# A two-layer streaming step: priority of PSUM copies for the steps between dependent products of indexer and attention

## The chip, the cores and the metric

The kernel runs on one core of a Trainium2 chip. The engines are PE (TensorE, matrix products; PEld is its weight load), DVE (VectorE), ACT (ScalarE), POOL (GpSimd) and SP (SyncE, which issues loads). The metric is the device time of one execution in microseconds.

## The reference

The program computes one inference step of a hybrid encoder with 2 layers of width 1024, for 512 prompt positions and 32 positions of a running stream with 1024 cached ones, in float32. A layer is:

```python
h = rms_norm(x, g_mix)
z = h @ w_in
...
q = rope(rms_norm(q.reshape(B, T, N_HEADS, HEAD_DIM), q_gain), pos)
...
qi = rope(qi.reshape(B, T, N_IDX, IDX_DIM), pos)
ki = rope(ki[:, :, None, :], pos)[:, :, 0, :]
wi = wi * IDX_W_SCALE
...
x = x + jnp.concatenate([y_a, y_b, y_c], axis=-1) @ w_out
hf = rms_norm(x, g_ffn)
x = x + jnp.square(jax.nn.relu(hf @ w_up)) @ w_down
```

`y_a` is a spatial gate and `y_b` a short convolution; `y_c` is attention over the positions that an indexer picks:

```python
logits = jax.nn.relu(jnp.einsum('bqnd,bsd->bqns', qi, ki_all).astype(jnp.float32))
iscore = jnp.einsum('bqn,bqns->bqs', wi.astype(jnp.float32), logits)
...
_, sel = lax.top_k(iscore, k_top)
...
p = jax.nn.softmax(s, axis=-1)
o = jnp.einsum('bqhgk,bqkhd->bqhgd', p.astype(v_sel.dtype), v_sel)
```

There are 8 indexer heads of 32, 8 attention heads of 64 that share 4 key heads, and `k_top` is 128 for the prompt and 256 of 1056 for the running stream.

## The kernel before, in words

Positions are cut into blocks b = 0 to 3 of 128 prompt positions and b = 4, the 32 of the running stream (called the sample). A float32 product is made of three products of split operands, hi*hi, lo*hi and hi*lo (lines 258 to 260), so each weight tile is loaded by SP (`raw`), cast on ACT into `hi` (L226) and subtracted into `lo` on DVE or POOL (L227). Inputs and weights of a layer come in this order: the indexer's columns of `w_in`, then q (two halves, split on POOL), k, v (split on POOL), the mixers' columns, `w_out`, and the feed-forward part.

The indexer loops over the five blocks. `tok_gemm` gives a block's 296 columns in PSUM; DVE rotates them (L574) and adds the halves (L577); ACT and DVE split keys (`ks`, L584 and L586) and queries (`qs`, L598 and L600); PE transposes them and ACT copies them out (L590, L592, L608). For blocks 1 to 3 there follow eight products, one a head (L612), each with a Relu on ACT into a buffer of the group "tt", of which there are four (L614), and an accumulation with the head's weight on DVE (L616 for the first head, L618 for the others). For block 4 the sum over heads is a second product on PE: its weights `wsel` are transposed and copied by DVE in four pieces (L638), then three column ranges each take two products (L644), a Relu (L646) and two products with `wsel` (L647), and a copy (L648).

After that come the products for q, k and v, with rope (L456, L458), sums of squares (L661, L662), adds (L687, L706) and transposes whose copies are at L693 and L720. The masks of blocks 1 to 3 are made on DVE by 16 rounds of MAX8 and MATCH_REPLACE (L465, L466), that of the sample by a search digit by digit. `attend(b)` then makes, for two heads at a time, two score products (L754) into the two PSUM tiles of the group "l"; DVE adds the mask and takes the row maximum in one instruction (L761), which frees the tile; ACT takes the exponential; PE transposes the probabilities, ACT copies them (L780), and PE multiplies by the values (L784). The mixers' products (L428, L683 and others) are ready at the same time and lie between these.

What sets the order is the scheduler of the tile framework. Each instruction has a priority, its place in the program, and of the instructions whose inputs it takes as ready each engine gets the one with the lowest number. Two blocks of code shift that number for what is issued in them. Each engine's instructions stand in the order that results.

```python
PREP = -1000000
EVAC = -2000000
...
prep = Shift(tc, PREP)
evac = Shift(tc, EVAC)
```

`prep` is round loads, casts and splits of weights (L226, L227), so they go ahead of all plain work; `evac` is round copies out of PSUM behind the large products (L571, L660, L683, L703, L728 and others), and goes ahead of both. Steps named above that have neither keep the priority of their place: L577, the splits of `ks` and `qs`, the Relus, the whole branch of block 4, the row maximum and the copies of transposes.

Of the kernel before, what the change touches and what calls it, by code (L numbers as in the profile page):

```python
# [16 lines left out]
NT = 512  # L17
NS = 32
PAST = 1024
# [36 lines left out]
def kernel(  # L56
# [20 lines left out]
    def nm(s):  # L77
        cnt[0] += 1
        return f"{s}_{cnt[0]}"
# [16 lines left out]
    def psum(tag):  # L96
        return pp.tile([128, 512], F32, tag=tag, name=nm("ps" + tag), bufs=PBUFS[tag])
# [293 lines left out]
    for l in range(depth):  # L391
# [162 lines left out]
        for b in range(5):  # L554
# [22 lines left out]
            nc.vector.tensor_tensor(t1[r], t1[r], t2[r], op=ALU.add)  # L577
# [4 lines left out]
            ks = sp.tile([128, 4, 32], F32R, tag="ks", name=nm("ks"), bufs=1)  # L582
            for a in range(2):
                nc.scalar.copy(ks[r, a, :], t1[r, 256:288])  # L584
            for a in range(2):
                nc.vector.tensor_tensor(ks[r, 2 + a, :], t1[r, 256:288], ks[r, 0, :].bitcast(F32), op=ALU.subtract)  # L586
            pt = psum("l")
            tr(pt[:, :nr], ks[r].rearrange("p a e -> p (a e)"), idr[r, r])
            if b < 4:
                nc.scalar.copy(kiTp[:, b * 128:b * 128 + 128], pt[:, :128])  # L590
            else:
                nc.scalar.copy(kiTs[:, PAST:SK], pt[:, :32])  # L592
# [4 lines left out]
            for a in range(2):  # L597
                nc.scalar.copy(qs[r, :, 2 * a, :], qv)  # L598
            for a in range(2):
                nc.vector.tensor_tensor(qs[r, :, 2 * a + 1, :], qv, qs[r, :, 0, :].bitcast(F32), op=ALU.subtract)  # L600
            if b < 4:
                n = 128 * (b + 1)
                qiT = Q([128, 8, 128], F32R)
                for g in range(2):
                    pt = psum("l")
                    for k in range(4):
                        tr(pt[:, k * 128:k * 128 + 128], qs[:, 4 * g + k].rearrange("p a e -> p (a e)"), idr)
                    nc.scalar.copy(qiT[:, 4 * g:4 * g + 4, :].rearrange("p h t -> p (h t)"), pt)  # L608
                work = keep([128, n], f"work{b}") if b < 3 else work3
                for hd in range(8):  # L610
                    pl = psum("lld"[hd % 3])
                    nc.tensor.matmul(pl[:, :n], lhsT=qiT[:, hd, :], rhs=kiTp[:, :n], start=True, stop=True)  # L612
                    rl = T(n, "tt")
                    nc.scalar.activation(rl, pl[:, :n], AF.Relu)  # L614
                    if hd == 0:
                        nc.vector.tensor_scalar(work, rl, wi[:, 0:1], None, op0=ALU.mult)  # L616
                    else:
                        nc.vector.scalar_tensor_tensor(work, rl, wi[:, hd:hd + 1], work, op0=ALU.mult, op1=ALU.add)  # L618
                nc.vector.memset(work[0:64, n - 64:n], INADM)
                masks[b] = work  # L620
            else:
                pt = psum("l")
                for k in range(8):
                    tr(pt[:, k * 32:k * 32 + 32], qs[r, k].rearrange("p a e -> p (a e)"), idr[r, r])
                qiTs = kiTq[:, NT:]
                nc.scalar.copy(qiTs, pt[:, :256])

                dg = Q([128, 256])
                nc.vector.tensor_tensor(
                    dg[r].rearrange("p (h t) -> p h t", h=8),  # L630
                    wi[r].rearrange("p (h o) -> p h o", o=1).to_broadcast([32, 8, 32]),
                    idn[r, r].rearrange("p (o t) -> p o t", o=1).to_broadcast([32, 8, 32]), op=ALU.mult)
                wsel = keep([128, 2, 4, 32], "wsel")
                pt = psum("l")
                for g in range(2):
                    tr(pt[:, g * 32:g * 32 + 32], dg[r, g * 128:g * 128 + 128], idn[r, r])
                for a in range(4):
                    nc.vector.tensor_copy(wsel[:, :, a, :], pt[:, :64].rearrange("p (g t) -> p g t", g=2))  # L638
                work = works
                for c0, cn in ((0, 512), (512, 512), (1024, 32)):  # L640
                    pi = psum("l")
                    for g in range(2):
                        pl = psum("l")
                        nc.tensor.matmul(pl[:, :cn], lhsT=qiTs[:, g * 128:g * 128 + 128], rhs=kiTs[:, c0:c0 + cn], start=True, stop=True)  # L644
                        rl = T(cn, "tt")
                        nc.scalar.activation(rl, pl[:, :cn], AF.Relu)  # L646
                        nc.tensor.matmul(pi[:, :cn], lhsT=wsel[:, g].rearrange("p a t -> p (a t)"), rhs=rl, start=(g == 0), stop=(g == 1))  # L647
                    nc.scalar.copy(work[:, c0:c0 + cn], pi[:, :cn])  # L648
# [23 lines left out]
        for u in range(2):  # L672
            pieces = w_tok(C_Q + 256 * u, 256, ((0, 4), (4, 8)), nc.gpsimd)
            for b in range(5):
# [13 lines left out]
                if b < 4:  # L688
                    def turn_q(b=b, u=u, dst=dst):
# [3 lines left out]
                        nc.scalar.copy(qT[b][:, u].rearrange("p h t -> p (h t)"), pt[:, :256])  # L693
# [3 lines left out]
        for b in range(5):  # L697
# [16 lines left out]
            if b < 4:  # L714
                nc.gpsimd.dma_start(nk_p[l, 0, b * 128:b * 128 + 128].rearrange("t h e -> t (h e)"), kf)
                def turn_k(b=b, kf=kf):
# [3 lines left out]
                    nc.scalar.copy(kTp[:, :, b * 128:b * 128 + 128], pt[:, :256].rearrange("p (u t) -> p u t", u=2))  # L720
# [23 lines left out]
        def attend(b):  # L744
# [4 lines left out]
            def scores(u, hh):  # L749
# [7 lines left out]
                for j in range(2):  # L757
# [3 lines left out]
                    nc.vector.tensor_tensor_reduce(out=t, in0=p[j][:, :n], in1=masks[b], op0=ALU.add, op1=ALU.max, scale=1.0, scalar=-3e38, accum_out=mx[:, o])  # L761
# [10 lines left out]
            def values(u, hh, probs, po):  # L772
                for k0 in range(0, b + 1, 2):
# [6 lines left out]
                    nc.scalar.copy(t[:, :kn * 256], pt[:, :kn * 256])  # L780
# [428 lines left out]
```

## Time and profile before

| What | Value |
|---|---|
| Median of 3 runs | 1354.03 us (1351.96 to 1359.14) |
| Profiled execution | 1352.13 us |
| Its span, first to last instruction | 1350.1 us |
| Mean granted clock of PE | 0.980 of full speed |
| PE busy | 1303.9 us, 97% of the span |
| DVE busy | 1064.3 us, 79% |
| ACT busy | 748.4 us, 55% |
| POOL busy | 106.0 us, 8% |
| Share of PE in the chain that ended last | 82% |

Layer 0 runs from the start to some 675 us, layer 1 from there to the end; indexer and attention are at about 30 to 170 and 685 to 830 us. A busy PE is not PE at its peak: a product counts as busy for longer where the granted clock is lower. So the busy share is read together with the granted clock, and stage by stage. Times in the rows below are microseconds from the start of the span.

### The profile page before, as it was taken

How to read it: one execution, taken by the hardware profiler on the slowest of the kernel's cores; microseconds unless marked ns; L12 is line 12 of the kernel's file. 1: busy time of each engine (PE TensorE's matmuls, PEld its weight loads, DVE VectorE, ACT ScalarE, POOL GpSimd, SP SyncE). 2: the span in 40 equal slices, each digit the busy share in tenths (PEclk: the TensorE clock that was granted, in tenths of full speed). 3: DMA queues.
4: the chain of work that ended last, by engine and by line, in shares of the span. 5: the costliest groups of instructions: out<-in, count | busy, mean ns of one | idle time of the engine just before them, and what ended most of it. 6: DMA issues, size and time to landing. Idle time of an engine off the chain costs nothing.

```text
span 1350.1 us, 25832 instructions
## 1 busy us (share of the span) xinstructions
PE 1303.9 (97%) x10056; PEld 1212.9 (90%) x10056; DVE 1064.3 (79%) x2585; ACT 748.4 (55%) x1494; POOL 106.0 (8%) x109
## 2 busy tenths in 40 slices
PE   7888999999999999999997989999999999999998
PEld 6767886899999999999985878778999999999997
DVE  6989988657985967958989989865778679588695
ACT  5746797445634536445654469853555364463452
POOL 5213300001000000000022120000100000000000
PEclk7999899999999999999988989999999999999999
DMA  7124322223233243242221232202232323323322
GB/s 208 34 67 94 78 66 63 64 83 86 79 104 101 65 124 94 63 125 69 83 60 33 71 104 65 79 24 87 79 95 78 110 79 94 110 78 97 93 84 77
DMA packets 150801, 113.00 MB, mean 84 GB/s; under 512 B 7028, under 2 KB 147848, under 8 KB 150680
## 3 DMA queue, kind: packets, MB, share of 16 engines
q1 hardware_dynamic: 148040, 106.35, 26.4%
q0 software_dynamic: 2640, 5.01, 2.0%
q8 instruction: 79, 1.29, 0.4%
q14 instruction: 42, 0.34, 0.1%
HBM read 106.67 MB, written 4.67 MB: 82 GB/s over the span
## 4 chain that ended last, share of the span: by engine, by line
PE 82%; DVE 9%; issue 5%; DMA 2%; ACT 1%; POOL 0%; POOLq 0%; SPq 0%; DVEq 0%; ACTq 0%
PE psm L258 16%; PE psm L259 16%; PE psm L260 16%; PE psl L1076 13%; PE psd L1076 6%; PE pso L1076 3%; PE psl L754 3%; PE psx L106 2%; PE pso L784 2%; PE psd L106 1%; DMA ahi<-in_x_prompt_dram 1%; DVE lo L227 1%; PE psl L837 1%; DVE work L618 1%; DVE m L465 1%
## 5 line engine op out<-in xcount | busy, mean ns | idle before, releaser
L226 ACT CAST hi<-raw 128x1024 fp32r<-128x1024 f32 (+1 forms) x124 | 126.4, 1022 | 131.2 <-PE psm L259 75.6
L259 PE MATMUL psm<-h1lo,hi 128*128 128x288 f32 x640 | 190.2, 297 | 0.0
L258 PE MATMUL psm<-h1hi,hi 128*128 128x288 f32 x640 | 190.0, 297 | 0.1
L260 PE MATMUL psm<-h1hi,lo 128*128 128x288 f32 x640 | 189.5, 296 | 0.0
L227 DVE TENSOR_TENSOR lo<-raw,hi 128x1024 fp32r<-128x1024 f32 (+1 forms) x99 | 119.3, 1207 | 83.2 <-ACT hi L226 83.0
L258 PE MATMUL psm<-h0hi,hi 128*128 128x256 f32 x640 | 182.0, 284 | 0.0
L260 PE MATMUL psm<-h0hi,lo 128*128 128x256 f32 x640 | 181.4, 283 | 0.4 <-POOL lo L227 0.4
L259 PE MATMUL psm<-h0lo,hi 128*128 128x256 f32 x640 | 180.6, 282 | 0.0
L1076 PE MATMUL psl<-e,hi 128*128 128x272 f32 x768 | 151.5, 289 | 0.8 <-DVE x L1069 0.5
L1076 PEld LDWEIGHTS psl<-e,hi 128*128 128x128 f32 x768 | 121.5, 188 | 3.1 <-DVE x L1069 1.1
L260 PEld LDWEIGHTS psm<-h0hi,lo 128*128 128x128 f32 x640 | 120.6, 188 | 1.8 <-issue 0.9
L258 PEld LDWEIGHTS psm<-h1hi,hi 128*128 128x128 f32 x640 | 120.4, 188 | 1.4 <-issue 1.0
L259 PEld LDWEIGHTS psm<-h1lo,hi 128*128 128x128 f32 x640 | 120.3, 188 | 1.2 <-issue 1.0
L258 PEld LDWEIGHTS psm<-h0hi,hi 128*128 128x128 f32 x640 | 120.6, 189 | 0.8 <-issue 0.7
L259 PEld LDWEIGHTS psm<-h0lo,hi 128*128 128x128 f32 x640 | 120.6, 188 | 0.7 <-issue 0.7
L260 PEld LDWEIGHTS psm<-h1hi,lo 128*128 128x128 f32 x640 | 120.4, 188 | 0.6 <-issue 0.5
L243 ACT CAST hi<-t 128x512 fp32r<-128x512 f32 x128 | 78.4, 619 | 70.2 <-PE psl L1076 27.2
L227 POOL TENSOR_TENSOR lo<-raw,hi 128x1024 fp32r<-128x1024 f32 (+1 forms) x25 | 58.9, 2361 | 728.2 <-ACT hi L226 712.0
L1076 PE MATMUL psl<-e,lo 128*128 128x272 f32 x384 | 110.9, 289 | 0.0
L243 ACT CAST hi<-raw 128x512 fp32r<-128x512 f32 x96 | 59.6, 621 | 78.6 <-PE psl L1076 47.5
L244 DVE TENSOR_TENSOR lo<-t,hi 128x512 fp32r<-128x512 f32 x128 | 87.1, 687 | 8.5 <-ACT hi L243 5.0
L1048 ACT ACTIVATE t<-t 128x544 f32<-128x544 f32 x64 | 42.2, 659 | 70.0 <-DVE t L1047 70.0
(351 smaller groups left out, 3722.2 us busy)
## 6 DMA issues: line engine op xcount, KB each, us to landing
raw<-in_w_up_dram SPq DMA_DIRECT2D x64, 512.0 KB, 4.1
raw<-in_w_down_dram SPq DMA_DIRECT2D x64, 512.0 KB, 3.6
raw<-in_w_in_dram SPq DMA_DIRECT2D x36, 512.0 KB, 3.7
raw<-in_w_out_dram SPq DMA_DIRECT2D x8, 512.0 KB, 3.5
raw<-in_w_out_dram SPq DMA_DIRECT2D x32, 128.0 KB, 3.0
raw<-in_w_in_dram SPq DMA_DIRECT2D x8, 296.0 KB, 6.6
q<-in_cache_k_dram SPq DMA_DIRECT2D x4, 512.0 KB, 3.8
h1lo<-in_cache_v_dram SPq DMA_DIRECT2D x2, 1024.0 KB, 6.0
```

The costliest lines, as they stand in the source:

```text
L106: nc.tensor.transpose(out, in_, ident)
L226: nc.scalar.copy(hi, raw)
L227: (eng or nc.vector).tensor_tensor(lo, raw, hi.bitcast(F32), op=ALU.subtract)
L243: nc.scalar.copy(hi, src)
L244: nc.vector.tensor_tensor(lo, src, hi.bitcast(F32), op=ALU.subtract)
L258: nc.tensor.matmul(out, lhsT=st[0], rhs=mv[0], start=first, stop=False)
L259: nc.tensor.matmul(out, lhsT=st[0], rhs=mv[1], start=False, stop=False)
L260: nc.tensor.matmul(out, lhsT=st[1], rhs=mv[0], start=False, stop=last)
L754: nc.tensor.matmul(p[j][:, :n], lhsT=qT[b][e, u, hh, :], rhs=kTp[e, u, :n], start=True, stop=True)
L784: nc.tensor.matmul(po[64 * j:64 * j + 64, hh * 128:hh * 128 + 128], lhsT=Vp[:, k0 + k, (2 * u + j) * 64:(2 * u + j + 1) * 64], rhs=t[:, (2 ...
L1048: nc.scalar.activation(hidden[f], hidden[f], AF.Square)
L1076: nc.tensor.matmul(p[:, :EVEN], lhsT=st[a], rhs=mv[b], start=first and (k, a, b) == (0, 0, 0), stop=(k, a) == (3, 1), skip_group_check=True)
```

## The change

Steps of the indexer and the attention are put into `with evac:`. These are the add of the rope halves, both splits and their transposes and copies, the Relus of blocks 1 to 3, everything of block 4's branch, the copies of turned q and k, the row maximum of `attend`, and the copy of the transposed probabilities. The accumulations of L616 and L618, the sums of squares, the adds of q and k, the top-k and its masks keep the priority of their place, and so do `attend_sample`, the mixers and the feed-forward part. What is computed does not change. Line numbers behind the first edit shift: L577 becomes L578, L614 L619, L618 L623, L638 L644, L647 L653, L662 L668, L687 L693, L706 L713, L761 L770.

```diff
@@ -574,30 +574,33 @@
-            nc.vector.tensor_tensor(t1[r], t1[r], t2[r], op=ALU.add)
+            with evac:
+                nc.vector.tensor_tensor(t1[r], t1[r], t2[r], op=ALU.add)
...
-            ks = sp.tile([128, 4, 32], F32R, tag="ks", name=nm("ks"), bufs=1)
-            for a in range(2):
-                nc.scalar.copy(ks[r, a, :], t1[r, 256:288])
+            with evac:
+                ks = sp.tile([128, 4, 32], F32R, tag="ks", name=nm("ks"), bufs=1)
+                for a in range(2):
+                    nc.scalar.copy(ks[r, a, :], t1[r, 256:288])
...
+                if b < 4:
+                    nc.scalar.copy(kiTp[:, b * 128:b * 128 + 128], pt[:, :128])
+                else:
+                    nc.scalar.copy(kiTs[:, PAST:SK], pt[:, :32])
...
-            for a in range(2):
-                nc.scalar.copy(qs[r, :, 2 * a, :], qv)
-            for a in range(2):
-                nc.vector.tensor_tensor(qs[r, :, 2 * a + 1, :], qv, qs[r, :, 0, :].bitcast(F32), op=ALU.subtract)
+            with evac:
+                for a in range(2):
+                    nc.scalar.copy(qs[r, :, 2 * a, :], qv)
+                for a in range(2):
+                    nc.vector.tensor_tensor(qs[r, :, 2 * a + 1, :], qv, qs[r, :, 0, :].bitcast(F32), op=ALU.subtract)
@@ -605,13 +608,15 @@
-                    nc.scalar.copy(qiT[:, 4 * g:4 * g + 4, :].rearrange("p h t -> p (h t)"), pt)
+                    with evac:
+                        nc.scalar.copy(qiT[:, 4 * g:4 * g + 4, :].rearrange("p h t -> p (h t)"), pt)
...
-                    nc.scalar.activation(rl, pl[:, :n], AF.Relu)
+                    with evac:
+                        nc.scalar.activation(rl, pl[:, :n], AF.Relu)
@@ -619,33 +624,34 @@
             else:
-                pt = psum("l")
...
+                with evac:
+                    pt = psum("l")
...
+                    for a in range(4):
+                        nc.vector.tensor_copy(wsel[:, :, a, :], pt[:, :64].rearrange("p (g t) -> p g t", g=2))
...
+                            nc.scalar.activation(rl, pl[:, :cn], AF.Relu)
+                            nc.tensor.matmul(pi[:, :cn], lhsT=wsel[:, g].rearrange("p a t -> p (a t)"), rhs=rl, start=(g == 0), stop=(g == 1))
+                        nc.scalar.copy(work[:, c0:c0 + cn], pi[:, :cn])
@@ -690,7 +696,8 @@
-                        nc.scalar.copy(qT[b][:, u].rearrange("p h t -> p (h t)"), pt[:, :256])
+                        with evac:
+                            nc.scalar.copy(qT[b][:, u].rearrange("p h t -> p (h t)"), pt[:, :256])
@@ -717,7 +724,8 @@
-                    nc.scalar.copy(kTp[:, :, b * 128:b * 128 + 128], pt[:, :256].rearrange("p (u t) -> p u t", u=2))
+                    with evac:
+                        nc.scalar.copy(kTp[:, :, b * 128:b * 128 + 128], pt[:, :256].rearrange("p (u t) -> p u t", u=2))
@@ -758,7 +766,8 @@
-                    nc.vector.tensor_tensor_reduce(out=t, in0=p[j][:, :n], in1=masks[b], op0=ALU.add, op1=ALU.max, scale=1.0, scalar=-3e38, accum_out=mx[:, o])
+                    with evac:
+                        nc.vector.tensor_tensor_reduce(out=t, in0=p[j][:, :n], in1=masks[b], op0=ALU.add, op1=ALU.max, scale=1.0, scalar=-3e38, accum_out=mx[:, o])
@@ -777,7 +786,8 @@
-                    nc.scalar.copy(t[:, :kn * 256], pt[:, :kn * 256])
+                    with evac:
+                        nc.scalar.copy(t[:, :kn * 256], pt[:, :kn * 256])
```

The order of DVE in layer 0 round the copies of `wsel` (`raw` and `lo` are a weight tile, `e_44` block 3's accumulator and the sample's rotated q, `t_9..` and `psm` the rope of q), before:

```order
L618 SCALAR_TENSOR_TENSOR e_44_269<-t_695,wi_134_635,e_44_269 128x512
L638 COPY wsel_768<-psl_769 128x2x32
L618 SCALAR_TENSOR_TENSOR e_44_269<-t_700,wi_134_635,e_44_269 128x512
L456 TENSOR_TENSOR e_44_269<-psm_988,tab_59_365 32x2x2x64
L227 TENSOR_TENSOR lo<-raw_1185,hi 128x1024
L618 SCALAR_TENSOR_TENSOR e_44_269<-t_705,wi_134_635,e_44_269 128x512
L638 COPY wsel_768<-psl_769 128x2x32
L619 MEMSET e_44_269 64x64
L638 COPY wsel_768<-psl_769 128x2x32 x2
```

and with the change:

```order
L456 TENSOR_TENSOR t_979<-psm_950,tab_59_365 128x2x2x64
L458 TENSOR_TENSOR t_980<-psm_950,tab_60_368 128x2x2x32 x2
L456 TENSOR_TENSOR e_44_269<-psm_988,tab_59_365 32x2x2x64
L644 COPY wsel_768<-psl_769 128x2x32 x4
L458 TENSOR_TENSOR t_995<-psm_988,tab_60_368 32x2x2x32 x2
L623 SCALAR_TENSOR_TENSOR e_44_269<-t_690,wi_134_635,e_44_269 128x512
L227 TENSOR_TENSOR lo<-raw_1185,hi 128x1024
L623 SCALAR_TENSOR_TENSOR e_44_269<-t_695,wi_134_635,e_44_269 128x512
```

The four copies now stand together, ahead of the split and of the four last accumulations of block 3, which all stood ahead of the last copies before (the first of them just above the rows shown); adds and rope steps of q stand ahead of them.

The order of ACT in layer 1 round the first Relus of block 2 (the CAST of `raw` is a weight cast, of `psl` the copy of a transposed query), before:

```order
L226 CAST hi<-raw_8741 128x1024
L608 CAST q_8469<-psl_8470 128x512
L608 CAST q_8469<-psl_8476 128x512
L226 CAST hi<-raw_8745 128x1024
L226 CAST hi<-raw_8919 128x1024
L431 COPY t_8758<-psm_8749 128x256
L614 ACTIVATE t_8485<-psl_8483 128x384
L614 ACTIVATE t_8490<-psl_8488 128x384
L614 ACTIVATE t_8495<-psd_8493 128x384
L614 ACTIVATE t_8500<-psl_8498 128x384
```

and with the change:

```order
L619 ACTIVATE t_8400<-psl_8398 128x256
L612 CAST q_8469<-psl_8476 128x512
L619 ACTIVATE t_8485<-psl_8483 128x384
L601 CAST q_8566<-t_8549 128x8x32 x2
L619 ACTIVATE t_8490<-psl_8488 128x384
L619 ACTIVATE t_8495<-psd_8493 128x384
L226 CAST hi<-raw_8741 128x1024
L619 ACTIVATE t_8500<-psl_8498 128x384
L226 CAST hi<-raw_8745 128x1024
L431 COPY t_8758<-psm_8749 128x256
L226 CAST hi<-raw_8919 128x1024
L619 ACTIVATE t_8505<-psl_8503 128x384
```

The Relus, and splits of the next block, moved ahead of the weight casts.

The order of DVE in layer 0 at the row maxima of the first pair of score products (each is an ISA row and a read of its accumulator), before:

```order
L761 ISA t_1813,sa_1811<-psl_1806,mask_346 128x128
L761 ISA sa_1811 128x1
L227 TENSOR_TENSOR lo<-raw_2515,hi 128x1024
L458 TENSOR_TENSOR t_1380<-psm_1350,tab_63_378 128x4x32 x2
L662 TENSOR_REDUCE ss_185_814<-t_1334 128x4
L706 TENSOR_TENSOR t_1379<-t_1379,t_1380 128x256
L709 TENSOR_SCALAR sr_1339<-ss_185_814 128x12
L499 TENSOR_SCALAR ti_1597<-ti_1588 128x1
L501 TENSOR_TENSOR ti_1599<-ti_1588,bst 128x1
L762 SCALAR_TENSOR_TENSOR sa_1812<-sa_1811,rq_188_817 128x1
L662 TENSOR_REDUCE ss_186_815<-t_1384 128x4
L159 SCALAR_TENSOR_TENSOR sr_1343<-sr_1339,sr_1341 128x12
L761 ISA t_1819,sa_1811<-psl_1807,mask_346 128x128
```

and with the change:

```order
L770 ISA t_1813,sa_1811<-psl_1806,mask_346 128x128
L770 ISA sa_1811 128x1
L770 ISA t_1819,sa_1811<-psl_1807,mask_346 128x128
L770 ISA sa_1811 128x1
L227 TENSOR_TENSOR lo<-raw_2515,hi 128x1024
```

The second row maximum stood behind a weight split and nine smaller steps, and now follows the first.

## Rows read from the trace of the kernel before

**Rows 1.** Windows: busy us and instructions of PE, PEld, DVE, ACT, POOL; PEclk; DMA share, GB/s.

```profile
100.00:150.00 50.00, 45.00 (x339) 39.38 (x337) 46.85 (x166) 32.21 (x58) 18.98 (x25) 0.90 0.45 101
...
250.00:300.00 50.00, 49.71 (x419) 44.99 (x418) 27.61 (x71) 22.33 (x43) 0.00 (x0) 1.00 0.31 88
...
750.00:800.00 50.00, 44.31 (x361) 39.25 (x361) 48.26 (x175) 27.85 (x56) 12.48 (x14) 0.94 0.29 87
```

**Rows 2.** Waits of PE by line: us in total, times, longest us.

```profile
PE psl L647 <- DVE wsel L638: 8.8, 2, 4.7
PE psl L754 <- DVE sa L761: 8.0, 4, 2.2
PE psl L612 <- ACT t L614: 5.1, 2, 3.2
```

**Rows 3.** Timeline of PE, stalls: start, us, instruction, idle before it and its releaser.

```profile
53.88 0.45 PE L612 MATMUL psl<-e,q 128*128 128x384 f32 x1 [1.94 <-ACT t L614]
...
73.70 2.05 PE L647 MATMUL psl<-t,wsel 128*128 128x512 f32 x2 [4.05 <-DVE wsel L638]
...
113.75 0.49 PE L754 MATMUL psl<-e,qT 64*128 64x128 f32 x2 [2.20 <-DVE sa L761]
...
133.09 0.48 PE L754 MATMUL psl<-e,qT 64*128 64x128 f32 x2 [2.17 <-DVE sa L761]
...
715.19 0.54 PE L612 MATMUL psl<-e,q 128*128 128x384 f32 x1 [3.20 <-ACT t L614]
...
737.07 2.05 PE L647 MATMUL psl<-t,wsel 128*128 128x512 f32 x2 [4.72 <-DVE wsel L638]
...
794.05 0.79 PE L754 MATMUL psl<-e,qT 64*128 64x128 f32 x2 [2.07 <-DVE sa L761]
```

**Rows 4.** Windows over the time behind the stalls, columns as in rows 1.

```profile
73.70:77.10 3.40, 3.40 (x8) 1.83 (x9) 2.04 (x8) 1.36 (x4) 0.00 (x0) 0.50 0.00 0
114.65:118.05 3.40, 2.93 (x21) 2.05 (x14) 3.06 (x20) 2.31 (x6) 0.00 (x0) 0.50 0.60 166
135.10:142.00 6.90, 6.90 (x28) 6.00 (x29) 5.55 (x10) 3.57 (x6) 5.57 (x6) 0.51 0.93 188
715.40:718.80 3.40, 3.40 (x17) 3.40 (x17) 2.99 (x11) 3.04 (x10) 0.00 (x0) 0.50 0.00 0
735.90:742.70 6.80, 5.63 (x12) 2.32 (x12) 5.99 (x22) 1.71 (x4) 0.00 (x0) 0.50 0.00 0
793.90:800.70 6.80, 5.04 (x21) 3.39 (x21) 5.42 (x15) 3.13 (x5) 3.30 (x3) 0.50 0.54 141
```

**Rows 5.** Timeline of DVE round the wsel copies of layer 0, columns as in rows 3.

```profile
68.13 0.22 DVE L638 COPY wsel<-psl 128x64 f32<-128x64 f32 x1
68.32 0.75 DVE L618 SCALAR_TENSOR_TENSOR e<-t,wi,e 128x512 f32<-128x512 f32 x1
...
70.39 1.98 DVE L227 TENSOR_TENSOR lo<-raw,hi 128x1024 fp32r<-128x1024 f32 x1 [0.26 <-ACT hi L226]
...
73.06 0.23 DVE L638 COPY wsel<-psl 128x64 f32<-128x64 f32 x1
...
73.80 0.75 DVE L687 TENSOR_TENSOR t<-t,t 128x256 f32<-128x256 f32 x2
74.47 0.42 DVE L456 TENSOR_TENSOR t<-psm,tab 128x256 f32<-128x256 f32 x1
74.80 0.48 DVE L458 TENSOR_TENSOR t<-psm,tab 128x128 f32<-128x128 f32 x2
```

**Rows 6.** Timeline of DVE: two adds of two SBUF tiles, one in each layer.

```profile
110.95 2.47 DVE L706 TENSOR_TENSOR t<-t,t 128x256 f32<-128x256 f32 x1
...
709.90 3.88 DVE L577 TENSOR_TENSOR t<-t,t 32x288 f32<-32x288 f32 x1
```

**Rows 7.** Timeline of POOL: two weight splits in layer 1.

```profile
708.75 4.70 POOL L227 TENSOR_TENSOR lo<-raw,hi 128x1024 fp32r<-128x1024 f32 x2
```

**Rows 8.** Timeline of ACT: two weight casts in layer 1.

```profile
706.09 2.00 ACT L226 CAST hi<-raw 128x1024 fp32r<-128x1024 f32 x2
```

More of the change, by code (lines that the diff above doesn't have):

```diff
@@ L596 @@
             qv = t1[r, :256].rearrange("p (h e) -> p h e", h=8)
-            for a in range(2):
-                nc.scalar.copy(qs[r, :, 2 * a, :], qv)
-            for a in range(2):
-                nc.vector.tensor_tensor(qs[r, :, 2 * a + 1, :], qv, qs[r, :, 0, :].bitcast(F32), op=ALU.subtract)
+            with evac:
+                for a in range(2):
+                    nc.scalar.copy(qs[r, :, 2 * a, :], qv)
+                for a in range(2):
+                    nc.vector.tensor_tensor(qs[r, :, 2 * a + 1, :], qv, qs[r, :, 0, :].bitcast(F32), op=ALU.subtract)
             if b < 4:
@@ L621 @@
             else:
[L622 to L641, printed above, removed]
-                    for g in range(2):
[L643 to L648, printed above, removed]
+                with evac:
+                    pt = psum("l")
+                    for k in range(8):
+                        tr(pt[:, k * 32:k * 32 + 32], qs[r, k].rearrange("p a e -> p (a e)"), idr[r, r])
+                    qiTs = kiTq[:, NT:]
+                    nc.scalar.copy(qiTs, pt[:, :256])
+                    dg = Q([128, 256])
+                    nc.vector.tensor_tensor(
+                        dg[r].rearrange("p (h t) -> p h t", h=8),
+                        wi[r].rearrange("p (h o) -> p h o", o=1).to_broadcast([32, 8, 32]),
+                        idn[r, r].rearrange("p (o t) -> p o t", o=1).to_broadcast([32, 8, 32]), op=ALU.mult)
+                    wsel = keep([128, 2, 4, 32], "wsel")
+                    pt = psum("l")
+                    for g in range(2):
+                        tr(pt[:, g * 32:g * 32 + 32], dg[r, g * 128:g * 128 + 128], idn[r, r])
+                    for a in range(4):
+                        nc.vector.tensor_copy(wsel[:, :, a, :], pt[:, :64].rearrange("p (g t) -> p g t", g=2))
+                    work = works
+                    for c0, cn in ((0, 512), (512, 512), (1024, 32)):
+                        pi = psum("l")
+                        for g in range(2):
+                            pl = psum("l")
+                            nc.tensor.matmul(pl[:, :cn], lhsT=qiTs[:, g * 128:g * 128 + 128], rhs=kiTs[:, c0:c0 + cn], start=True, stop=True)
+                            rl = T(cn, "tt")
+                            nc.scalar.activation(rl, pl[:, :cn], AF.Relu)
+                            nc.tensor.matmul(pi[:, :cn], lhsT=wsel[:, g].rearrange("p a t -> p (a t)"), rhs=rl, start=(g == 0), stop=(g == 1))
+                        nc.scalar.copy(work[:, c0:c0 + cn], pi[:, :cn])
```

8 lines of the change are left out of this document (2 added, 6 removed).

## The prediction

> **What bounds the kernel now.** I read the windows of the span first, to find where TensorE (PE) is short of work. Late in the layer there is nothing to win: from 250 to 300 us PE is busy 49.7 of 50 us, at the full clock, with 419 products at about 0.12 us each [rows 1]. The windows that hold the indexer and the start of the attention look otherwise: from 100 to 150 us PE is busy 45.0 us at a mean granted clock of 0.90, and from 750 to 800 us 44.3 us at 0.94. In the same windows VectorE (DVE) is busy 46.9 and 48.3 of 50 us. So in these stages DVE is nearly full and PE waits now and then; what stands in front of what in DVE's queue decides.
>
> Second came the waits of PE by line, to see for what it waits [rows 2]. Three groups lead: the sum over heads of the sample's indexer (L647) waits 8.8 us in two waits for the `wsel` copies on DVE (L638); the attention's score products (L754) wait 8.0 us in four waits for the row maximum on DVE (L761) that frees their PSUM tile; and the prompt's index scores (L612) wait 5.1 us in two waits for the Relu on ScalarE (ACT, L614). All three releasers are steps that the change raises. Together they are 21.9 us.
>
> [...] So **the ceiling** of what the change can give is 21.9 + 13.7 = 35.6 us.
>
> Last, the timelines of DVE, ACT and POOL say why the releasers were late [rows 5 to 7]. In layer 0 the first of the four `wsel` copies ran at 68.13, so their source lay ready in PSUM by then; the next came at 73.06. Between them stood accumulations (L618, 0.75 us each) and a weight split (L227, 1.98 us). That is order, not data, and the order is what the change touches. But the other cause is not order: the add of L577 took 3.88 us at 709.90, where an L456 over nearly as many columns takes 0.42 [rows 5, 6], and it ended with the two splits that POOL ran in 4.70 us from 708.75 [rows 7]; the add of L706 took 2.47 us at 110.95 [rows 6].
>
> **The change part by part.** No instruction is added or removed; only the order moves, in the indexer and attention of both layers, so no term comes from work done. I cost the edits by the stalls they reach.
>
> Layer 0. *Relu and rope add:* in the old order two top-k rounds stand on DVE in front of block 2's first accumulation, which frees a Relu's buffer; in the new order none does. The stall at 53.88 goes: -1.9. *wsel:* four L618 (3.0 us) and the L227 (1.98) move behind the copies, 5.0 us; two L687 (0.75), an L456 (0.42), two L458 (0.48) and an L662 (256 columns too, so about an L456) come in front, 2.1 [rows 5]. The copies are 2.9 us earlier, and PE has, by its order, nine more 256-column products and seven of L428 ahead of the first waiting product, at 0.12 us each [rows 1] some 1.9 us of cover. 4.8 is over 4.05, so stall and slow clock go: -4.05 - 1.70 = -5.75. *Row maximum at 113.75:* it waited behind the L706 that ran 2.47 us; that add stands ahead of it in the new order too. I take 0, between 0 and -3.7. *Row maximum at 133.09:* top-k rounds go behind it, but DVE has little idle time from which it could come earlier. Half of 2.17 + 3.45: -2.8, between 0 and -5.6. *The debt:* the 5.0 us moved behind `wsel` are done later, in a window where DVE idles 50 - 46.9 = 3.1 us. I give back 3 us, between 0 and 5; it is not all of it, since from 250 to 300 us DVE idles 22.4 us and part of the top-k can wait that long. Layer 0: -1.9 - 5.75 - 2.8 + 3 = **-7.4**.
>
> Layer 1. *Relu:* three weight casts (L226, 1.0 us each [rows 8]) stood in front of the five Relus; now most stand behind, and the last score product stands behind other products. The stall at 715.19 goes, -3.20 - 1.70 = -4.9. The casts feed the splits on POOL, on which the q products wait; those come later. That price the trace has not: it lies between 0 (the casts hidden as now) and 4.7 (both splits in the open). I take 1.5, three late Relus and a half cast, nearer the lower end because the new order puts index scores of blocks 2 and 3 ahead of the q products. *wsel:* the same move, larger; the stall and its slow clock are 4.72 + 2.82 = 7.5 us. A POOL split now starts close to these copies, and one costs a blocked DVE 2.35 us (half of 4.70): -5.2, between 0 and -7.5. *Row maxima at 794.05 and after:* the four L754 waits of 8.0 us leave 1.6 us for the one not shown; with 2.07 and the clock's 2.52 it is 6.2 us, and again half: -3.1. *Debt:* 3. Layer 1: -3.4 - 5.2 - 3.1 + 3 = **-8.7**.
>
> The other raised steps (turned q and k, transposed probabilities, splits of ks and qs) release none of the waits above; where they come earlier, products already queued cover them: nothing. On SP's queue only the loads of the cached keys move, behind some loads of w_out; they are read in attend_sample, behind all prompt blocks. On POOL only stores change places. Nothing for either.
>
> The sum is -16.1 us. The profiled execution took 1352.1 us (span 1350.1), which is 1.9 below the median of the three runs, near the fastest. On the median: 1354.0 - 16.1 = **1338 us**.
>
> [...] The row shows an add of two SBUF tiles that ends with POOL's two splits [rows 6, 7]. [...]
>
> **The rivals.** *(b) All stalls go.* For it: the three groups are all released by raised steps, and nothing replaces them in the order. Against: the DVE windows at 94 to 97%. 1354.0 - 35.6 = 1318. *(c) The stalls only move.* For it: DVE is so full from 100 to 150 and from 750 to 800 us that PE's next need finds it late whatever comes first; POOL's splits take their 2.4 us of DVE wherever they fall. Then the gains of `wsel` and row maxima (about 5.75 + 2.8 + 5.2 + 3.1 = 16.9) come back as waits in the attention, and some 2 us remain: 1350 to 1355. Against: the stalls at 53.88 and 73.70, 6.0 of the 21.9 us, hung on order alone. That the change doesn't do what it says belongs here too; but the new order has the four copies in one row. *(d) Slower, through attend(2) and attend(3).* The top-k of blocks 2 and 3 is not raised, so all raised work goes in front of it, and its mask is what the last prompt blocks of the attention wait for. The mixers' products, which filled PE during these blocks, are all placed before them now. If the top-k comes late, PE stands with nothing in its queue. Four such waits of a POOL split's length, 2.35 us, each followed by 3.4 us at half clock (1.7), cost 16.2 us; with only layer 0's `wsel` (5.75) kept, that is +10.5: about 1364. It decides once the postponed DVE work (5.0 us) outgrows DVE's idle time before these blocks (3.1 us in the window above). Against: I count part of the 5.0 us as needed later than that.
>
> **How the numbers follow.** My forecast gets 0.47, with a range of its own: no debt and the halved terms whole gain 28 us, debts of 5 and the halved terms at nothing gain 6, so 1326 to 1348. (b) 0.17, (c) 0.22, (d) 0.14. A difference under 0.5%, 6.8 us, can't be told from none here. Faster: forecast and (b), with a little of (c), 0.65; same 0.21; slower 0.14. The range leaves out (d) and keeps the rest: 1318 to 1355.
>
> **What would show it.** Right: PE's waits for `wsel` and for the Relu under 1 us in all, no half clock round 74 and 737 us, the order's top-k work seen on DVE after 140 us. Half right: the waits for the row maximum still there, next to POOL's splits. Wrong: new waits of PE for DVE in the attention of blocks 2 and 3, with the clock at 0.50 behind them, or waits for POOL's `lo` of over 2 us at the first q products.

## The result, and the profile after

The median went from 1353.24 us (5 runs, 1350.58 to 1359.14) to 1342.27 us (5 runs, 1338.02 to 1344.19). The ratio is 0.9921, with a 95% interval of 0.9898 to 0.9944: faster by 8 to 14 us. I had forecast 1338 in a range of 1318 to 1355. The sign is right, the size is two thirds of the forecast, and in the two traces the layers are not alike at all.

The page after, its span and its busy times, to be held against the table of before:

```profile
span 1341.1 us, 25813 instructions
...
PE 1299.7 (97%) x10054; PEld 1212.9 (90%) x10056; DVE 1062.6 (79%) x2585; ACT 750.5 (56%) x1496; POOL 103.8 (8%) x109
```

PE is busy 4.2 us less and idle 4.8 us less. DVE has the same to do. To part the layers, I take the first long wait of layer 1, for the split of its first normalised input. Timeline of PE, before and after:

```profile
683.27 0.40 PE L260 MATMUL psm<-hi,h0lo 128*128 128x296 f32 x1 [0.99 <-DVE h0lo L288]
```

```profile
674.83 0.40 PE L260 MATMUL psm<-hi,h0lo 128*128 128x296 f32 x1 [0.99 <-DVE h0lo L288]
```

Layer 0 is 8.4 us shorter. From there to the end of the span it was 1350.1 - 683.3 = 666.8 us and is 1341.1 - 674.8 = 666.3: **in these two executions layer 1 gained half a microsecond**, though its stalls were the larger ones. There is one trace of each kernel, and the times of one kernel lie up to 9 us apart before and 6 us after, so a difference of some microseconds in a layer is a reading of single executions.

Waits of PE by line after, to be read against [rows 2]:

```profile
PE psl L762 <- DVE sa L770: 6.3, 4, 2.2
...
PE psm L259 <- POOL lo L227: 3.9, 4, 1.6
PE psl L106 <- ACT t L619: 3.5, 3, 2.7
...
PE psx L197 <- DVE t L196: 2.1, 1, 2.1
```

The 8.8 us of waits for `wsel` and the 5.1 us of L612 are gone. But the waits for the row maximum are at 6.3 of 8.0 us, and there are new ones, or longer ones: for POOL's `lo`, for the Relu at the next transposes, and for a small DVE step (L196). The timeline of PE gives the longer ones their places, as in [rows 3]:

```profile
58.10 0.56 PE L197 MATMUL psx<-t,ones 128*128 128x128 f32 x2 [2.15 <-DVE t L196]
...
126.54 1.00 PE L762 MATMUL psl<-e,qT 64*128 64x128 f32 x4 [1.19 <-DVE sa L770]
...
131.09 1.01 PE L762 MATMUL psl<-e,qT 64*128 64x128 f32 x4 [0.98 <-DVE sa L770]
...
702.19 0.39 PE L259 MATMUL psm<-lo,h0hi 128*128 128x256 f32 x1 [1.35 <-POOL lo L227]
...
705.72 0.39 PE L259 MATMUL psm<-lo,h0hi 128*128 128x256 f32 x1 [1.61 <-POOL lo L227]
...
709.77 0.28 PE L106 MATMUL psl<-idr,ks 128*128 128x128 f32 x1 [2.66 <-ACT t L619]
...
764.52 0.49 PE L762 MATMUL psl<-e,qT 64*128 64x128 f32 x2 [2.17 <-DVE sa L770]
...
787.70 0.70 PE L762 MATMUL psl<-e,qT 64*128 64x128 f32 x4 [1.93 <-DVE sa L770]
```

The windows over the time behind them, as in [rows 4]:

```profile
58.40:61.80 3.40, 3.40 (x15) 3.12 (x14) 2.79 (x11) 1.68 (x3) 0.00 (x0) 0.50 0.00 0
126.70:136.90 10.20, 9.22 (x41) 6.89 (x42) 9.77 (x29) 5.16 (x11) 6.77 (x9) 0.50 0.80 175
710.40:713.80 3.40, 3.18 (x15) 2.89 (x16) 3.17 (x10) 2.34 (x7) 0.00 (x0) 0.51 0.01 2
...
sum 27.20, PE 26.00 PEld 21.06 DVE 24.99 ACT 14.56 POOL 7.33; mean PE 5.20 PEld 4.21 DVE 5.00 ACT 2.91 POOL 1.47
```

These are three of five stretches, and the sum of all five: 27.2 us at a granted clock of 0.50 to 0.51, against 30.7 before. So the half clock got only a little shorter; it stands at other places.

The larger windows, as in [rows 1]:

```profile
100.00:150.00 50.00, 45.41 (x347) 38.75 (x345) 47.14 (x173) 32.71 (x63) 18.69 (x26) 0.90 0.39 87
...
250.00:300.00 50.00, 49.84 (x423) 45.55 (x422) 31.22 (x74) 24.36 (x48) 2.41 (x1) 1.00 0.24 67
...
750.00:800.00 50.00, 45.33 (x346) 40.05 (x344) 44.88 (x169) 32.49 (x59) 10.10 (x12) 0.90 0.31 90
```

From 100 to 150 us hardly anything changed. DVE now idles 18.8 us from 250 to 300 instead of 22.4, but that is not postponed top-k: layer 0's last step of it (L466) starts at 186.9 us, and started at 183.7 before. What DVE has more of in this window is the splitting and squaring of normalised inputs (L288, L275), which come earlier now, and POOL runs a split beside them.

### The profile page after: what moved, and what is told of

The parts are those of the page before. It is cut to its first block, busy times and chain, and to the rows that moved or that the text cites. A ratio compares the mean times of both kernels' runs of the same rounds, so it can differ in the third digit from the quotient of the medians.

```text
span 1341.1 us, 25813 instructions
## 1 busy us (share of the span) xinstructions
PE 1299.7 (97%) x10054; PEld 1212.9 (90%) x10056; DVE 1062.6 (79%) x2585; ACT 750.5 (56%) x1496; POOL 103.8 (8%) x109
## 4 chain that ended last, share of the span: by engine, by line
PE 81%; DVE 10%; issue 3%; DMA 3%; ACT 2%; POOL 0%; POOLq 0%; SPq 0%; DVEq 0%; ACTq 0%
PE psm L258 16%; PE psm L259 15%; PE psm L260 15%; PE psl L1086 13%; PE psd L1086 6%; PE pso L1086 3%; PE psl L762 2%; PE psx L106 2%; PE pso L794 2%; PE psd L106 1%; DVE work L623 1%; DMA ahi<-in_x_prompt_dram 1%; DMA raw<-in_w_down_dram 1%; DVE work L466 1%; PE psl L653 1%
## 5 line engine op out<-in xcount | busy, mean ns | idle before, releaser
L227 DVE TENSOR_TENSOR lo<-raw,hi 128x1024 fp32r<-128x1024 f32 (+1 forms) x99 | 118.6, 1200 | 81.7 <-ACT hi L226 81.4
L227 POOL TENSOR_TENSOR lo<-raw,hi 128x1024 fp32r<-128x1024 f32 (+1 forms) x25 | 58.1, 2325 | 734.2 <-ACT hi L226 718.0
```

The source lines that it names most:

```text
L227: (eng or nc.vector).tensor_tensor(lo, raw, hi.bitcast(F32), op=ALU.subtract)
```

## The experiments

After the result I held this. **Theory A:** the raised order helps at `wsel`, and what is left of the stalls comes from POOL's weight splits, which stop DVE wherever they fall. **Theory B:** DVE is simply full, so the order decides little. Below, the lock is a name for what was measured and for no mechanism: a DVE instruction that ran beside POOL's work and took longer than its like, as the two adds of [rows 6] did, 2.47 us where the add of that line and shape took 0.42 at 115.48 (before), and 3.88 where the same add took 0.44 at 692.71 in e4. All ratios are to the kernel before, measured on the same chip, with their 95% intervals.

| Run | Ratio | Interval | Median, us |
|---|---|---|---|
| the change | 0.9921 | 0.9898 to 0.9944 | 1342.3 |
| e1, only block 4's branch raised | 0.9914 | 0.9895 to 0.9934 | 1340.1 |
| e2, the change with plain Relus | 0.9930 | 0.9908 to 0.9952 | 1342.4 |
| e3, only the attention's steps raised | 0.9994 | 0.9978 to 1.0010 | 1351.5 |
| e4, the change, splits on DVE | 0.9847 | 0.9821 to 0.9872 | 1331.3 |
| e5, before, splits on DVE | 0.9865 | 0.9845 to 0.9886 | 1334.7 |
| e6, the change, POOL's casts first | 0.9884 | 0.9861 to 0.9908 | 1337.8 |
| e7, accumulations raised too | 0.9919 | 0.9898 to 0.9940 | 1342.6 |
| e8, e1 with splits on DVE | 0.9871 | 0.9848 to 0.9893 | 1334.8 |
| e9, e4 with idle work on POOL | 1.0037 | 1.0020 to 1.0053 | 1357.1 |
| e10, e4 with all splits on DVE | 0.9857 | 0.9842 to 0.9871 | 1331.8 |
| e11, the change, k on POOL as well | 0.9973 | 0.9958 to 0.9988 | 1348.6 |
| e12, e4 with the gate raised | 0.9858 | 0.9837 to 0.9879 | 1333.9 |

### Which raised step is it (e1, e2, e3)

e1 is the kernel before with the whole `else` branch of block 4 in `with evac:`, and nothing else.

> The kernel before, with block 4's branch alone raised (wsel copies, its products, Relus and copy). Theory A (order, then POOL's splits): the two waits for wsel (8.8 us) and the half clock behind them (1.7 + 2.8 us) go, part of it comes back through DVE work that is done later: 5 to 11 us faster than before, ratio 0.992 to 0.996, so most of what the whole change gives. Theory B (DVE is full, the order doesn't matter): under 4 us faster, the stall turns up at the next need of PE.

It gains 9 to 14 us, as much as the whole change or a little more. Waits of PE by line of e1:

```profile
PE psl L755 <- DVE sa L762: 8.0, 3, 3.3
PE psl L612 <- ACT t L614: 5.1, 2, 3.2
...
PE psl L648 <- DVE wsel L639: 1.5, 1, 1.5
```

Here the waits for L612 and for the row maximum stand as they were, 5.1 and 8.0 us, and of 8.8 us for `wsel` 1.5 are left; 2.4 us, in three waits, are for the Relus of that branch (L647). Theory A's range of 5 to 11 us was a little short. So the other raised steps of the change together add nothing that can be measured.

e2 takes the Relus of blocks 1 to 3 out of the change:

```diff
-                    with evac:
-                        nc.scalar.activation(rl, pl[:, :n], AF.Relu)
+                    nc.scalar.activation(rl, pl[:, :n], AF.Relu)
```

> The changed kernel with the Relus of blocks 1 to 3 put back to the priority of their place, so that in layer 1 the three weight casts stand ahead of them again. Theory A: the waits of PE for POOL's lo at 702 and 706 us (1.35 and 1.61 us) shrink to under 1 in all and the 2.66 us behind the Relu at 710 go too, since POOL's splits come earlier; 2 to 5 us faster than the change (some 1338). Theory B: within 2 us of the change. If the Relu's priority was worth what I gave it (1.9 + 4.9 us), 4 us or more slower than the change (some 1346).

The time is that of the change, so neither my 6.8 us for the Relus nor theory A's 2 to 5 us came out; theory B's sentence did. The waits did not do what theory A said either: those for `lo` in layer 1 are 1.02 + 0.86 us, not under 1, and one of 1.41 us for the Relu stays. The layers differ more than the sum. Timeline of PE of e2:

```profile
48.38 0.28 PE L106 MATMUL psl<-idr,ks 128*128 128x128 f32 x1 [2.91 <-ACT t L618]
...
680.90 0.40 PE L260 MATMUL psm<-hi,h0lo 128*128 128x296 f32 x1 [1.30 <-DVE h0lo L288]
```

Layer 1 begins at 680.9 and takes 656.2 of the 1337.1 us: it is 10 us shorter than in the change, in an execution that was the fastest of e2's six. Some 3 us of the 10 have nothing to do with the Relus: the change ran 6.8 us at half clock (0.50) at the start of layer 1, from 676.2 us, where a product of 296 columns counts as busy for 0.45 us, and e2 ran at the full clock there, with 0.30 us for such a product. Layer 0 is 6 us longer than in the change, and its stall of 2.91 us at 48.38 follows three splits that POOL now runs one behind the other, as its timeline shows:

```profile
39.66 7.32 POOL L227 TENSOR_TENSOR lo<-raw,hi 128x1024 fp32r<-128x1024 f32 x3 [1.77 <-ACT hi L226]
```

So the Relu's priority moves POOL's splits, and the sum over both layers stays. That the new places are the reason why one layer is longer and the other shorter is read from one trace each and not shown.

e3 is the kernel before with `with evac:` round L693, L720, L761 and L780 alone.

> The kernel before, with the attention's steps alone raised (row maximum, copies of probabilities, of turned q and of turned k). Theory A: the row maxima waited mainly behind adds that POOL's splits held, and order doesn't move those: the waits for the row maximum stay at 5 us or more, time 0 to 4 us below before, ratio 0.997 to 1.000. The prediction counted 5.9 us for them (2.8 + 3.1). Theory B: the same as before.

Nothing: the interval holds 1. The wait for the row maximum is what it was, 7.9 us in three waits (L756 in that kernel) against 8.0.

### POOL's splits (e4, e5)

e4 is the change with the splits of the indexer's, q and v weights on DVE; e5 has the same edit in the kernel before.

```diff
-        idxw += w_tok(C_IDX, 296, ((2, 4), (4, 6), (6, 8)), nc.gpsimd if l else None)
+        idxw += w_tok(C_IDX, 296, ((2, 4), (4, 6), (6, 8)))
...
-            pieces = w_tok(C_Q + 256 * u, 256, ((0, 4), (4, 8)), nc.gpsimd)
+            pieces = w_tok(C_Q + 256 * u, 256, ((0, 4), (4, 8)))
...
-        pieces = w_tok(C_V, 256, ((0, 4), (4, 8)), nc.gpsimd)
+        pieces = w_tok(C_V, 256, ((0, 4), (4, 8)))
```

> The changed kernel with the splits of the indexer's, q and v weights on DVE instead of POOL: 15 splits of about 1.2 us each, 18 us more work for DVE in both layers, and no split on POOL there. Theory A: the locked DVE instructions (some 2 us each, about 9 of them in these stages, 20 us) go as well, and with them the waits for the row maximum and for lo: 2 to 8 us faster than the change (1334 to 1340). Theory B: DVE is the bound and has more to do: 5 to 15 us slower than the change (1347 to 1357).

e4 is 11 us faster than the change and 21 faster than before, beyond the upper end of what theory A asked. Fifteen splits more on DVE, and its busy time falls. Line 1 of the page of e4 (in e5 DVE has 2600 instructions too and is busy 1056.9 us):

```profile
PE 1295.6 (98%) x10054; PEld 1208.0 (91%) x10056; DVE 1054.0 (79%) x2600; ACT 743.9 (56%) x1491; POOL 69.6 (5%) x94
```

DVE has 2600 instructions instead of 2585 and is busy 1054.0 instead of 1062.6 us, though its weight splits (L227) alone went from 118.6 to 135.7 us. The groups of DVE instructions show where that comes from; first the change, then e4 (the last number is the idle time before):

```profile
L623 DVE SCALAR_TENSOR_TENSOR work<-t,wi,work 128x256 f32<-128x256 f32 (+1 forms) x28 | 24.7, 884 | 0.6
...
L713 DVE TENSOR_TENSOR t<-t,t 128x256 f32<-128x256 f32 (+1 forms) x10 | 7.6, 763 | 0.0
```

```profile
L623 DVE SCALAR_TENSOR_TENSOR work<-t,wi,work 128x256 f32<-128x256 f32 (+1 forms) x28 | 15.0, 545 | 0.3
...
L713 DVE TENSOR_TENSOR t<-t,t 128x256 f32<-128x256 f32 (+1 forms) x10 | 4.2, 419 | 0.1
```

An accumulation takes 0.545 us on average instead of 0.884, the add of k 0.419 instead of 0.763. Theory B, which had DVE's load for its reason, falls.

> The kernel before (nothing raised) with the splits of the indexer's, q and v weights on DVE, as in e4. Theory A (POOL's splits lock DVE and cost by themselves, the order of wsel costs by itself): 6 to 14 us faster than before, 1339 to 1347, and the two waits for wsel stay, together 6 us or more. Theory C (the locks only hurt where the priorities put a raised step behind them): within 4 us of before.

e5 gains 18 us by its ratio with nothing raised, more than theory A's 14; theory C, which had it within 4 us of before, falls. Its waits of PE:

```profile
PE psl L754 <- DVE sa L761: 7.0, 4, 4.7
PE psl L106 <- DVE q L629: 4.2, 2, 2.9
...
PE psl L647 <- ACT t L646: 1.4, 2, 0.7
```

The two waits for `wsel` (L647) did not stay, against my expectation: what is left of that chain is 4.2 us at its head (L629) and 1.4 us for the Relus. So DVE reached the copies in time though nothing was raised. The stall that the change removes was late work of DVE, and part of that lateness was POOL's. But 5.6 us of waits are left in that chain where 8.8 were, so most of the 18 us came elsewhere. The waits for the row maximum stay at 7.0 us; the longest, 4.7 at 777.54, comes behind one of four splits that POOL keeps in the attention (2.33 us from 773.02), beside which a split on DVE took 3.39 us.

### Where the splits fall (e6, e7, e8)

e6 gives the casts and splits that go to POOL a priority above the raised steps.

```diff
+            if eng is not None:
+                tc.cur_priority += 2 * PREP
             nc.scalar.copy(hi, raw)
             (eng or nc.vector).tensor_tensor(lo, raw, hi.bitcast(F32), op=ALU.subtract)
+            if eng is not None:
+                tc.cur_priority -= 2 * PREP
```

> The changed kernel with the casts and splits of the pieces that POOL splits given a priority above the raised steps, so that they no longer stand behind Relus. Theory A as I hold it now: the waits for lo in layer 1 (1.35 and 1.61 us) go under 1 us in all, but the splits still lock DVE, only at other places, so the time is within 3 us of the change (1339 to 1345). If the late casts were the cause of layer 1's lost gain, 4 us or more faster than the change (under 1338).

1337.8 us is 4.5 under the change, and the intervals meet, so whether e6 is faster than the change stays open. Its trace parts the layers as e2's does:

```profile
49.55 0.37 PE L106 MATMUL psl<-idr,ks 128*128 128x128 f32 x1 [3.87 <-ACT t L623]
...
679.34 0.41 PE L264 MATMUL psm<-hi,h0lo 128*128 128x296 f32 x1 [1.25 <-DVE h0lo L292]
```

Layer 1 takes 1336.7 - 679.3 = 657.4 us, 9 less than in the change, and layer 0 is 4.5 longer, with a wait of 3.87 us at 49.55 for a Relu whose buffer DVE freed late. The last sentence of the expectation blames the late casts for layer 1's lost gain, and its time of under 1338 was just met. The waits bear it out only in part: those for `lo` are down from 2.96 to 0.57 us in layer 1, but one of 2.94 us for the Relu still stands at 710.76, with 3.4 us at half clock behind it. So the 9 us are not accounted for.

e7 raises the accumulations L621 and L623 as well.

> The changed kernel with the accumulations of blocks 1 to 3 raised as well, which come before block 4 in the program, so the wsel copies stand behind them again. If the gain hangs on wsel standing ahead of the accumulations (theory A), a wait for wsel of 2 us or more a layer comes back and the time is 3 to 8 us over the change (1345 to 1350). If DVE's total work is what counts (theory B), the same as the change, within 2 us.

The wait for `wsel` comes back, in layer 0:

```profile
PE psl L654 <- DVE wsel L645: 2.5, 1, 2.5
```

The time is that of the change all the same: the wait that theory A expected came in one layer, and its price in the total did not. In this run raising more moved waits to other places, and the sum stayed.

e8 is e1 with the edit of e4.

> Block 4's branch alone raised (e1) and the splits on DVE (e4). If the two parts add and the other raised steps give nothing: 11 us under e1, so 1327 to 1332, the same as e4 or 2 us better. If the raised Relus and row maxima gain once no lock spoils them: 3 us or more slower than e4 (1334 or more).

1334.8 us, the same as e5 that raises nothing. So `wsel`'s place in the queue, worth 12 us while POOL splits weights, is worth nothing that I can measure once it doesn't. e4 is 3.5 us under e8, which the second sentence expected; their intervals overlap, so whether Relus and row maxima gain then stays open.

### Is it the lock or the lateness (e9, e11, e10, e12)

In the change POOL took 2.36 us for a split (at 761.61) that DVE did in 1.22 (at 764.60), so e4 could have gained because `lo` comes sooner. e9 keeps the splits on DVE, and lets POOL do the same subtractions into a scratch tile:

```diff
+            if eng is True:
+                idle = sp.tile([128, 512], BF16, tag="idle", name=nm("idle"), bufs=1)
+                v = idle[:, :a * c // 2].rearrange("p (k c) -> p k c", k=a // 2)
+                for k in (0, a // 2):
+                    nc.gpsimd.tensor_tensor(v, raw[:, k:k + a // 2], hi[:, k:k + a // 2].bitcast(F32), op=ALU.subtract)
+                eng = None
...
```

The three calls that e4 edits pass `True` for the engine here.

> e4 (the change, splits on DVE), and POOL does the same subtractions once more into a scratch tile that nobody reads, two halves for each of the 15 pieces. PE never waits for POOL here, so only what POOL's reading does to DVE is left. Theory A (the lock): DVE instructions stretched by 1 us and more come back, and the time is 8 to 20 us over e4 (1339 to 1351). If POOL was only a slow place for a split that PE waits for, within 3 us of e4 (1331).

1357.1 us, 26 over e4, and more than theory A's 20: slower than the kernel that the study began with, for work whose result nobody reads. The page of e9, to be held against e4's:

```profile
PE 1306.4 (97%) x10056; PEld 1215.7 (90%) x10056; DVE 1073.3 (79%) x2600; ACT 745.0 (55%) x1491; POOL 117.3 (9%) x124
```

The same 2600 instructions of DVE take 1073.3 us instead of 1054.0. The same place in layer 1, POOL and DVE of e9, then DVE of e4:

```profile
703.23 11.50 POOL L231 TENSOR_TENSOR idle<-raw,hi 128x512 bf16<-128x512 f32 x6
```

```profile
706.04 4.42 DVE L233 TENSOR_TENSOR lo<-raw,hi 128x1024 fp32r<-128x1024 f32 x2
710.38 1.48 DVE L629 SCALAR_TENSOR_TENSOR work<-t,wi,work 128x256 f32<-128x256 f32 x1
```

```profile
693.18 2.36 DVE L227 TENSOR_TENSOR lo<-raw,hi 128x1024 fp32r<-128x1024 f32 x2
695.46 0.48 DVE L623 SCALAR_TENSOR_TENSOR work<-t,wi,work 128x256 f32<-128x256 f32 x1
```

Two splits on DVE take 4.42 us beside POOL's six, and 2.36 us without; the accumulation behind them 1.48 and 0.48. One reservation: the scratch work also keeps a loaded weight tile in use for longer, and POOL ran 48.1 us of it where the splits of the change were some 34 (58.1 in all, less the 24.1 of e4), so 26 us is more than the splits themselves cost. PE waits for POOL's remaining `lo` for 0.4 us in all, as in e4; that the cost is there without PE waiting for POOL is what this run shows.

e11 is the other direction, k's weights on POOL too, four splits more (`w_tok(C_K, ...)` with `nc.gpsimd`).

> The changed kernel with the k weights split on POOL as well: four splits more that lock DVE, at the same stage. Theory A: e4 took 15 splits from POOL for some 11 us, 0.7 us each; four more cost 2 to 6 us (1344 to 1349). Theory B: DVE has 4.9 us less to do, so 0 to 4 us faster than the change.

6.3 us over the change, 1.6 us a split, a little more than theory A's 2 to 6 us. Theory B had it 0 to 4 us faster.

e10 moves the remaining ten splits of POOL to DVE as well.

> e4 with the remaining ten weight splits of POOL on DVE too (the spatial gate's and the first of the feed-forward part). DVE has idle time there and PE hardly waits: theory A expects the stretched steps of L288 (2.3 us instead of 0.5, three a layer) to go, and no more than 3 us less time than e4 (1328 to 1332).

1331.8 us, no different from e4. The stretched steps of L288 are gone, as expected: the longest takes 0.95 us instead of 2.33. So the lock of these ten splits costs nothing that I can measure. Idle time of DVE can explain that for the six near 300 and 950 us, but not for the other four, which stood in the attention (at 121, 140, 768 and 787 us in e4); why these cost nothing stays open.

e12 was a try at the largest wait that e4 has left, by raising L926 and L952 to L956.

> e4 with two more kinds of DVE step raised that free buffers of the group g for the short convolution: the gate's last product (L926) and the convolution's five steps (L952 to L956). In e4 PE waited 3.38 and 3.12 us for DVE's L935, which had no buffer; if these are what it lacked, the waits go under 2 us in all, with the half clock behind them: 3 to 8 us under e4 (1323 to 1328). If DVE just has that much to do there, the waits move to the attention of blocks 2 and 3 and the time stays within 2 us of e4.

It is not faster: 2.6 us over e4, with intervals that overlap. The waits of PE of e4 and of e12:

```profile
PE psm L258 <- DVE t L935: 6.5, 2, 3.4
```

```profile
PE psd L106 <- DVE q L528: 8.4, 2, 4.3
```

6.5 us of waits went, and 8.4 us came at the next place where PE needs DVE in that stage (e10, where the gate is not raised, has one wait of 4.3 us there too): the rival of the expectation, that the waits move, if not to the place it named. No version is faster than e4, 1331.3 us.

## Why the prediction was right, and where it was not

**What bounds the kernel** held: DVE nearly full, PE waiting at a few places, and a granted clock of 0.50 to 0.51 behind them, 30.7 us of it before and 27.2 after. The 13.7 us for it in the ceiling, and the 1.70, 1.47, 3.45, 1.70, 2.82 and 2.52 us in it that my sums and ranges take up, were my estimate: half of PE's busy time in the six windows of [rows 4]. No run shows that this half is saved; what the trace of before shows is that a product of 256 columns began every 0.21 us at half clock and every 0.12 us at the full one:

```profile
141.15 0.41 PE L259 MATMUL psm<-lo,h0hi 128*128 128x256 f32 x1
141.36 0.41 PE L260 MATMUL psm<-hi,h0lo 128*128 128x256 f32 x1
...
291.06 0.28 PE L258 MATMUL psm<-ahi,hi 128*128 128x256 f32 x1
291.18 0.28 PE L259 MATMUL psm<-alo,hi 128*128 128x256 f32 x1
```

**wsel** was right, and was all of the gain that can be measured. In layer 0 the four copies now stand together, with the accumulations and the weight split behind them; timeline of DVE after:

```profile
70.85 0.62 DVE L644 COPY wsel<-psl 128x64 f32<-128x64 f32 x4 [0.47 <-PE psl L106]
...
72.02 0.75 DVE L623 SCALAR_TENSOR_TENSOR e<-t,wi,e 128x512 f32<-128x512 f32 x1
72.69 1.22 DVE L227 TENSOR_TENSOR lo<-raw,hi 128x1024 fp32r<-128x1024 f32 x1
```

PE waits for `wsel` in neither layer, and no half clock follows there: the granted clock is 1.00 from 70 to 80 us and from 723 to 741. I had counted 5.75 + 5.2 us for it and a debt of 3 us a layer against it, so 5 net; e1 measured some 12 net. The other 11.2 us of my sum, for Relus and row maxima, did not show up (e1, e2, e3). That the total came near is in good part luck: one term too small stood against two that brought nothing.

**The Relu step** is the first term that failed, in layer 1 above all. I took its late casts at 1.5 us, between 0 and 4.7, and found 4.9 for the stall, so -3.4 in all. Here is what stands there now: DVE, ACT and POOL.

```profile
700.22 2.23 DVE L578 TENSOR_TENSOR t<-t,t 32x288 f32<-32x288 f32 x1
702.49 5.92 DVE L623 SCALAR_TENSOR_TENSOR work<-t,wi,work 128x256 f32<-128x256 f32 x2
```

```profile
703.00 0.49 ACT L619 ACTIVATE t<-psl 128x384 f32<-128x384 f32 x1 [0.78 <-DVE work L623]
708.44 0.49 ACT L619 ACTIVATE t<-psd 128x384 f32<-128x384 f32 x1 [4.94 <-DVE work L623]
```

```profile
703.29 4.68 POOL L227 TENSOR_TENSOR lo<-raw,hi 128x1024 fp32r<-128x1024 f32 x2
```

POOL's two splits in a row came behind the Relus, at 703.3 to 708.0, and fell on the accumulations: two of them took 5.92 us, the second alone 5.52, through both of POOL's splits. Those free the Relus' buffers, so a Relu waited to 708.44, and PE with it. In layer 1 the waits for `lo` are 1.35 + 1.61 us where one of 0.70 was, then come 2.66 us for the Relu and 3.4 us at half clock (1.6): about 6.5 us, against the 4.9 that the step won. Read from this one trace it is +1.6 instead of -3.4. One of my own signs of being wrong came, waits of over 2 us for POOL's `lo` at the first q products (1.35 + 1.61), and the waits for the Relu, 3.5 us in all, are not under 1. I had bounded the casts by their own time in the open, and left out what the splits they feed would do to DVE at their new place. e2 and e6, where the casts come earlier, have layer 1 shorter by 9 to 10 us and layer 0 longer by 4.5 to 6, with the reservations above.

Layer 0 has the same. The stall at 53.88 is gone, my -1.9, and a new one of 2.15 us stands at 58.10, with 3.4 us at half clock (1.7) behind it. It waits for a small step (L196) that DVE reaches late, behind an accumulation that ran beside a split; DVE, then POOL:

```profile
54.11 2.76 DVE L623 SCALAR_TENSOR_TENSOR work<-t,wi,work 128x384 f32<-128x384 f32 x1
```

```profile
54.07 2.38 POOL L227 TENSOR_TENSOR lo<-raw,hi 128x1024 fp32r<-128x1024 f32 x1 [5.59 <-ACT hi L226]
```

The next accumulations of that shape take 0.62 us.

**The row maxima** I had at -2.8 and -3.1. e3 measured 0 to within 3 us. The step that failed here is "half": I said that DVE had little idle time to come earlier from, and then still booked half. After the change one wait of 2.17 us follows an add (L713, 2.12 us at 762.14) beside a split of POOL (2.36 us from 761.61), as before; in layer 0 a stretch of 10.2 us at half clock begins at a wait of 1.19 us and holds the next, of 0.98, where 6.9 us followed one of 2.17.

**The debt**, 3 us a layer, no run shows: e1, which postpones that work, gained more than I had counted for `wsel` without any debt. The windows from 250 to 300 us hold no top-k before or after, so none of it waited for the idle time there.

**The rivals.** (c), the stalls only move, held for everything except `wsel`, and I had priced it by DVE's load. The load was the wrong reason: e4 and e5 gave DVE fifteen splits more and were faster. (d) didn't come: no wait of PE in the attention of blocks 2 and 3 is over 1 us. **POOL's splits** were what mattered. I had one of them at 2.35 us of DVE's time, half of the 4.70 of [rows 7], and booked it once, at layer 1's `wsel`; moving fifteen of POOL's twenty-five splits to DVE gave 18 us by e5, more than the order was worth. What the runs show is durations: two splits on DVE took 4.42 us beside POOL's idle work in e9 and 2.36 without it in e4, and in the change an accumulation took 2.76 us beside a split of 2.38, where the next ones of that shape took 0.62. Why DVE takes longer there, no run shows.

## What to carry to other kernels

Before reordering an engine that is late, look at its instructions that take far longer than their like: here VectorE's other instructions took some 26 us less once fifteen splits had left GpSimd (in e4 it was busy 8.6 us less with 17.1 us more of splits), and raising steps did not reach that. Work handed to GpSimd to relieve VectorE can cost VectorE more than it saves, here some 26 us for 17.1, and the busy times of the two show it only when one compares durations within a group. And count a raised step with all that it pushes back and with what that will then fall on: the raised Relus pushed back weight casts, POOL's splits followed these, and the step gained nothing that can be measured.

## What the runs showed of the hardware that I had not expected

- Taking fifteen instructions of 1.2 us from GpSimd onto VectorE lowered VectorE's busy time by 8.6 us (1062.6 to 1054.0).
- Thirty subtractions on GpSimd whose results nobody reads, 48.1 us in all, made the kernel 26 us slower and VectorE's same 2600 instructions 19.3 us longer.
- In the change one accumulation on VectorE took 5.52 us, through two GpSimd splits in a row, though it began 0.4 us ahead of the first.
- After the change the granted clock was at 0.50 to 0.51 for 27.2 us in these stages against 30.7, though PE was idle 4.8 us less in all: a stall of 1.19 us before 126.5 us was followed by 10.2 us at a granted clock of 0.50, with a second stall of 0.98 us inside it. No stall in these stages before, up to 4.72 us long, had more than 6.9 us behind it.
